# A streaming encoder layer on one core: roots turned on TensorE, a first load in two pieces, and another order in the last unit

## The chip, the cores and the metric

The kernel runs on one core of a Trainium2 chip. The metric is the device time of one execution in microseconds. Engine names: PE is TensorE (PEld its weight loads), DVE is VectorE, ACT is ScalarE, POOL is GpSimd, SP is SyncE. SP here does nothing but issue DMAs, in the order of its one queue; SPq and ACTq are the DMA-issuing sides of the engines.

## The reference

One layer for two groups of requests that share weights: a prompt of 2048 frames and 32 sample frames with cached state, width 1024, hidden width 2816, all in float32. In short:

```
h = RMSNorm(x); z = h @ W_in             # [pool u | q | f | i | g], 512 columns each
A = per-group map of (trailing mean over 2/4/8/16 frames - frame)
B = HGRN2 recurrence, 4 heads x 128, in chunks; per-head RMSNorm; SiLU(g) gate
x += RMSNorm(concat(A, B) @ W_out)
x += RMSNorm((SiLU(RMSNorm(x) @ W_gate) * (RMSNorm(x) @ W_up)) @ W_down)
outputs: y_prompt, y_sample, new pool rows and new states of both groups
```

The root of the first RMSNorm, 1 / sqrt(mean(x^2) + eps), is a number per frame. It is what the words "roots" below mean.

## The kernel before, in words

The prompt is worked off in two halves of 1024 frames; the sample frames ride with the second half. Each half goes through: values (the `i` columns), four heads (`head_products`, with the recurrence `hgrn` run as a background task), four pool groups, the output projection (`project`, in two token groups of 512), and the gate and up products (`gate_up`). After both halves the down products of both run in `down`.

Every float32 product is made from two rounded parts of each operand, high and low, as three matmuls (high x high, high x low, low x high); ACT casts the high part and DVE subtracts to get the low part. Gate, up and down use a seven-product scheme on 2 x 2 blocks: a unit has the products 1 to 7, and `order_of` writes down in which order they run. Products that share a PSUM bank (`u.x` of 1, 6, 5, 3; `u.y` of 7, 4) follow one another in it, each after DVE or ACT has read the last state. In `down` each unit adds its products into four quarters of two token tiles `acc[t]` and `acc[t + 4]`: product 2 completes the left half of tile t, 5 and 4 the two halves of tile t + 4, and 3 the right half of tile t. When both halves of a tile are complete, a root is taken on POOL and DVE scales both halves (`done`). For all units but the last the result is added to the output in DRAM by a POOL DMA; for the last unit DVE multiplies each completed half by the norm's weight (`fg`), scales it and adds the residual, and plain stores end the program.

What sets the order: PE's instructions are in the order of the program text, where background tasks (`Task`, `poll`) are stepped between matmuls by a clock of estimated PE time, `Pace.t`; a `yield n` asks for the next step n ns later. The queues of DVE, ACT, POOL and SP are ordered by a scheduler that estimates when each instruction is ready, so the same edit can move instructions on engines that it doesn't name. In the first values stage (`first_values`) the text sets the order of all engines.

Places that the change touches. `later_stats` (L466) takes the roots of the second half's 1024 frames during the first half: `st[:, 24:32]` holds them as 128 partitions x 8, and L489 stores them into the DRAM row `roots`, from where L521 broadcasts them to all partitions, hundreds of us later. `first_values` (L560) starts the program: 12 idle matmuls, the loads of x and of the first weights, and `unscaled` and `split`, which make the operands of the first products. `flush` (L1414) is the task that works off the hidden tiles' splits (`hidden`: `hhi`, `hlo`, `hs`) that are left when a half's gate and up products end. `gb` products are the small in-chunk products of a head, 64 in a group.

Of the kernel before, what the change touches and what calls it, by code (L numbers as in the profile page):

```python
# [16 lines left out]
P = 128  # L17
# [61 lines left out]
def body(tc, ins, outs, cst):  # L79
    nc = tc.nc  # L80
    ctx = ExitStack()
    with ctx:
# [113 lines left out]
        def tick(ns):  # L196
            Pace.t += ns
# [267 lines left out]
        def later_stats(S):  # L465

            st = S.st
            for i in range(NCH):
                for c in range(2):
                    x = t2("xtl")  # L470
                    r0 = S.tok0 + i * P
                    nc.sync.dma_start(out=x, in_=x_p[r0:r0 + P, c * 512:c * 512 + 512])
                    sumsq(x, P, st[:, 2 * i + c:2 * i + c + 1])
                    del x
                yield 20000.0
            xs = t2("xsl", [NS, 512]), t2("xsl", [NS, 512])
# [12 lines left out]
            nc.sync.dma_start(out=roots[0, 0:HALF].rearrange("(i p) -> p i", p=P), in_=st[:, 24:32])  # L489
            nc.sync.dma_start(out=roots[0, HALF:TMAX].rearrange("(p i) -> p i", i=1), in_=st[0:NS, 35:36])  # L490

        def scaled_channels(S, tg):
# [67 lines left out]
        def first_values(S):  # L560


            idle = small("idle", [P, 1], bufs=1)
            nc.scalar.activation(idle, ones[:, 0:1], AF.Copy)
            bank = axbank("idle")
            for _ in range(12):
                mm(bank[:, 0:P], ones, ones, True, True, 0.0)
            front_loads(S)
            S.xT[0] = [ztile("xT", [P, 2, 512]) for _ in range(4)]
            for kp in range(4):  # L570
                channel_load(S, 0, 2 * kp, 2 if kp else 1)
                raws(kp + 1)
                if kp == 0:
                    channel_load(S, 0, 1, 1)
            nc.sync.dma_start(out=cons[:, 0:C_VEC], in_=cst[:, 0:C_VEC])
            xg = {}

            def unscaled(k):
                x, c = S.xT[0][k // 2][:, k % 2], xtile("xg", [P, 2, 512])
                nc.scalar.activation(c[:, 0], x, AF.Copy, scale=g_pre[:, k:k + 1])  # L580
                nc.vector.scalar_tensor_tensor(c[:, 1], x, g_pre[:, k:k + 1], c[:, 0].bitcast(F32), ALU.mult, ALU.subtract)
                xg[k] = c[:, 0], c[:, 1]

            token_tiles(S, 1)
            S.xT[1] = [ztile("xT", [P, 2, 512]) for _ in range(4)]
            for kp in range(4):
                channel_load(S, 1, 2 * kp, 2)
                raws(kp + 5)
            token_tiles(S, 0)
            unscaled(0)  # L590
            ahead(1)
            unscaled(1)
            pss = value_tiles(S)
            for k in range(0, KD, 2):
                _, hi, lo = take(0)
                if k + 2 < KD:
                    unscaled(k + 2)
                    ahead(Stream.used + 1)
                    unscaled(k + 3)
                else:  # L600
                    ahead(Stream.used + 1)
                if k == 4:
                    token_stats(S, 1)
                for kk in range(2):
                    ah, al = xg.pop(k + kk)
                    if k + kk == 0:
                        for n, (a, b) in enumerate(((ah, hi[0]), (al, hi[0]), (ah, lo[0]))):
                            for i in range(4):
                                mm(pss[i], a[:, i * P:(i + 1) * P], b, n == 0, False, rcost(512))
                    else:  # L610
                        for i in range(4):
                            value_products(pss, i, ah, al, i * P, hi[kk], lo[kk], False, k + kk == KD - 1)
                    if k + kk == KD - 3:
                        later = scaled_channels(S, 1)
                        next(later)
                        next(later)
            for i in range(4):
                (nc.vector.tensor_copy if i % 2 else nc.scalar.copy)(S.vt[i], pss[i])
            pss = value_tiles(S)
            for k in range(0, KD, 2):  # L620
                _, hi, lo = take(0)
                next(later, 0)
                ahead(Stream.used + 1)
                if k == 2:
                    token_stats(S, 0, range(2))
                    next(later, 0)
                elif k == 4:
                    token_stats(S, 0, range(2, 4))
                    gate_bounds()
                elif k == 6:  # L630
                    for i in range(4):
                        if i % 2:
                            nc.vector.tensor_scalar(S.vt[i], S.vt[i], S.rs[0][i], None, ALU.mult)
                        else:
                            nc.scalar.activation(S.vt[i], S.vt[i], AF.Copy, scale=S.rs[0][i])
                for kk in range(2):
                    if k + kk == KD - 1:
                        earlier = scaled_channels(S, 0)
                        next(earlier)
                    ah, al = S.hT[k + kk]  # L640
                    for i in range(4):
# [493 lines left out]
        def order_of(n, lead):  # L1135
# [13 lines left out]
                    out += [(m - 1, 4), (m - 1, 3)]  # L1149
                out += [(m, 6), (m, 2), (m, 7), (m, 5)]  # L1150
            if not lead:
                return out + [(n - 1, 4), (n - 1, 3)]
            a, b = n - 2, n - 1
            return out + [(a, 1), (a - 1, 4), (a - 1, 3), (b, 1)] + [(m, p) for p in (6, 2, 7, 5, 4, 3) for m in (a, b)]

# [45 lines left out]
        def gate_up(S, on_last):  # L1201
# [212 lines left out]
            def flush():  # L1414
                while jobs:
                    job()
                    yield 1400.0

            Task(flush())

# [75 lines left out]
        def down(halves):  # L1496
# [38 lines left out]
            def half_done(t, dh, direct):  # L1535
                cs = slice(dh * 512, dh * 512 + 512)
                f = acc[t][:, cs]
                if t not in stats:
                    xh = None
                    if direct:  # L1540
                        xh = ztile("x1r", [P, D])
                        nc.sync.dma_start(out=xh, in_=x1_rows(t * P, P))
                    stats[t] = [new_stat(), [], xh]
                st, seen, xh = stats[t][0:3]
                sumsq(f, P, st[:, dh:dh + 1])
                seen.append(dh)
                if direct:
                    fg = t2("fg")
                    nc.vector.tensor_tensor(fg, f, gpf[0][:, cs], ALU.mult)
                    stats[t].append((dh, fg))  # L1550
                if len(seen) == 1:
                    first_half(st, P, dh)
                else:
                    rstd_of(st, P, True, nc.gpsimd, dh)
                    pending.append((slot[0] + (1 if direct else 4), lambda: done(t, direct)))

            def done(t, direct):
                f, rs, xh, fg = acc[t], stats[t][0][:, 3:4], stats[t][2], stats[t][3:]
                rows = slice(t * P, (t + 1) * P)
                for i in range(2):  # L1560
                    ds = slice(i * 512, i * 512 + 512)
                    if direct:
                        nc.vector.scalar_tensor_tensor(f[:, ds], dict(fg)[i], rs, xh[:, ds], ALU.mult, ALU.add)
                        (nc.scalar if i else nc.sync).dma_start(out=outs[0][0, rows, ds], in_=f[:, ds])
                    else:
                        nc.vector.scalar_tensor_tensor(f[:, ds], f[:, ds], rs, gpf[0][:, ds], ALU.mult, ALU.mult)
                if not direct:
# [182 lines left out]
```

## Time and profile before

| | |
|---|---|
| median of 3 runs | 2109.58 us (2109.41 to 2110.47) |
| profiled execution | 2110.55 us |
| its span | 2108.8 us |
| mean granted clock of TensorE | 0.996 |
| PE busy | 2081.5 us, 99% |
| PEld, DVE, ACT, POOL busy | 80%, 68%, 39%, 13% |
| DMA engines | 152 GB/s on the mean |

The rows below are of the profiled execution. Times are us from the start of its span. An instruction of a timeline has its start, its duration, its engine and line, what it writes and reads, and in brackets how long the engine stood idle before it and what ended that; "issue" means that nothing that the profile shows ended it. Consecutive like instructions are merged (x2, x64), with one duration for all.

### The profile page before, as it was taken

How to read it: one execution, taken by the hardware profiler on the slowest of the kernel's cores; microseconds unless marked ns; L12 is line 12 of the kernel's file. 1: busy time of each engine (PE TensorE's matmuls, PEld its weight loads, DVE VectorE, ACT ScalarE, POOL GpSimd, SP SyncE). 2: the span in 40 equal slices, each digit the busy share in tenths (PEclk: the TensorE clock that was granted, in tenths of full speed). 3: DMA queues.
4: the chain of work that ended last, by engine and by line, in shares of the span. 5: the costliest groups of instructions: out<-in, count | busy, mean ns of one | idle time of the engine just before them, and what ended most of it. 6: DMA issues, size and time to landing. Idle time of an engine off the chain costs nothing.

```text
span 2108.8 us, 34100 instructions
## 1 busy us (share of the span) xinstructions
PE 2081.5 (99%) x13117; PEld 1690.4 (80%) x13117; DVE 1423.5 (68%) x2302; ACT 831.6 (39%) x1659; POOL 283.4 (13%) x387
## 2 busy tenths in 40 slices
PE   9999899999999999999999999999999999999998
PEld 8788688888888887778878788888888778888876
DVE  6565575797777778456575687767666856566587
ACT  6444344654444445233333664444444521011032
POOL 1132302200000000022231210000000301110134
PEclk9999999999999999999999999999999999999999
DMA  9321142626555557310014524545455796776778
GB/s 322 111 72 51 34 150 96 194 86 176 162 155 155 150 175 229 112 45 25 23 36 162 188 93 130 156 141 148 147 148 151 241 311 207 225 225 196 223 224 215
DMA packets 394242, 321.07 MB, mean 152 GB/s; under 512 B 19144, under 2 KB 321472, under 8 KB 394080
## 3 DMA queue, kind: packets, MB, share of 16 engines
q1 hardware_dynamic: 391632, 310.98, 47.9%
q0 software_dynamic: 2016, 7.34, 1.9%
q8 instruction: 104, 1.70, 0.3%
q10 hardware_dynamic: 432, 0.57, 0.1%
q14 instruction: 58, 0.48, 0.1%
HBM read 218.36 MB, written 100.47 MB: 151 GB/s over the span
## 4 chain that ended last, share of the span: by engine, by line
PE 88%; DVE 6%; issue 2%; DMA 1%; ACT 1%; POOL 1%; SPq 0%; DVEq 0%; POOLq 0%; ACTq 0%
PE gx L200 21%; PE mmb L200 15%; PE gy L200 10%; PE dx L200 10%; PE ops L200 10%; PE gz L200 5%; PE dy L200 5%; PE vps L200 3%; PE dz L200 2%; PE gb L200 1%; DVE acc L1533 1%; PE gw L200 1%; PE gsps L200 1%; PE ups L200 1%; PE tps L343 1%
## 5 line engine op out<-in xcount | busy, mean ns | idle before, releaser
L200 PE MATMUL gx<-fhi,wf 128*128 128x512 f32 x1376 | 387.3, 391 | 0.0
L200 PEld LDWEIGHTS gx<-fhi,wf 128*128 128x128 f32 x1376 | 256.6, 188 | 55.3 <-issue 3.0
L200 PE MATMUL gx<-flo,wf 128*128 128x512 f32 x688 | 213.0, 390 | 0.0
L200 PE MATMUL gy<-fhi,wf 128*128 128x512 f32 x704 | 201.8, 390 | 0.1
L200 PE MATMUL dx<-dhi,hst 128*128 128x512 f32 x640 | 185.3, 391 | 0.8 <-DVE acc L1533 0.6
L200 PE MATMUL mmb<-hTlo,whi 128*128 128x512 f32 x512 | 177.4, 407 | 0.0
L200 PE MATMUL mmb<-hThi,whi 128*128 128x512 f32 x512 | 166.4, 406 | 5.6 <-issue 5.6
L1533 DVE TENSOR_TENSOR acc<-dx,acc 128x512 f32<-128x512 f32 x168 | 115.0, 689 | 72.9 <-PE dx L200 72.1
L1256 DVE TENSOR_TENSOR wf<-s,wf 128x512 fp32r<-128x512 f32 x176 | 119.9, 687 | 60.6 <-ACT wf L1251 58.3
L200 PE MATMUL mmb<-hThi,wlo 128*128 128x512 f32 x512 | 159.9, 394 | 0.0
L200 PEld LDWEIGHTS gy<-fhi,wf 128*128 128x128 f32 x704 | 131.7, 188 | 28.5 <-DVE c L1355 0.8
L200 PEld LDWEIGHTS gx<-flo,wf 128*128 128x128 f32 x688 | 129.1, 188 | 27.0
L1251 ACT CAST wf<-s 128x512 fp32r<-128x512 f32 x176 | 108.3, 621 | 102.5 <-DVE s L1232 31.5
L200 PEld LDWEIGHTS dx<-dhi,hst 128*128 128x128 f32 x640 | 119.5, 188 | 30.0 <-issue 3.4
L1256 DVE TENSOR_TENSOR wf<-wraw,wf 128x512 fp32r<-128x512 f32 x132 | 89.6, 686 | 40.2 <-ACT wf L1251 40.2
L200 PEld LDWEIGHTS mmb<-hThi,whi 128*128 128x128 f32 x512 | 91.6, 189 | 27.3 <-issue 10.0
L200 PEld LDWEIGHTS mmb<-hTlo,whi 128*128 128x128 f32 x512 | 96.6, 189 | 21.1 <-issue 1.3
L200 PEld LDWEIGHTS mmb<-hThi,wlo 128*128 128x128 f32 x512 | 96.9, 189 | 19.5 <-issue 0.7
L1472 ACT CAST dhi<-t 128x1024 fp32r<-128x1024 f32 x20 | 20.6, 1052 | 232.2 <-DVE dlo L1473 163.7
L1251 ACT CAST wf<-wraw 128x512 fp32r<-128x512 f32 x132 | 80.8, 621 | 73.9 <-PE gx L200 37.4
L200 PE MATMUL gy<-flo,wf 128*128 128x512 f32 x352 | 108.7, 389 | 0.0
L200 PE MATMUL dy<-dhi,hst 128*128 128x512 f32 x320 | 98.6, 389 | 1.1 <-DVE acc L1533 1.1
(327 smaller groups left out, 3998.0 us busy)
## 6 DMA issues: line engine op xcount, KB each, us to landing
hst<-hdFalse SPq DMA_DIRECT2D x140, 256.0 KB, 3.0
hst<-hdTrue SPq DMA_DIRECT2D x140, 256.0 KB, 3.0
wraw<-in_w_gate_dram SPq DMA_DIRECT2D x50, 512.0 KB, 4.2
wraw<-in_w_up_dram SPq DMA_DIRECT2D x50, 512.0 KB, 4.0
hdFalse<-hhi SPq DMA_DIRECT2D x77, 256.0 KB, 2.3
hdFalse<-hlo SPq DMA_DIRECT2D x77, 256.0 KB, 2.5
hdTrue<-hhi SPq DMA_DIRECT2D x77, 256.0 KB, 2.6
hdTrue<-hlo SPq DMA_DIRECT2D x77, 256.0 KB, 2.5
```

The costliest lines, as they stand in the source:

```text
L200: nc.tensor.matmul(out, l, r, start=start, stop=stop, skip_group_check=more)
L343: nc.tensor.transpose(ps[:, c:c + P], xn[:, (2 * kp + kk) * P:(2 * kp + kk + 1) * P], ident)
L1251: nc.scalar.copy(wf[:, 0], getattr(M, src) if isinstance(src, str) else src)
L1256: nc.vector.tensor_tensor(wf[:, 1], getattr(M, src) if isinstance(src, str) else src, wf[:, 0].bitcast(F32), ALU.subtract)
L1472: nc.scalar.copy(hi, src)
L1533: nc.vector.tensor_tensor(dst, ps, dst, ALU.add)
```

## The change

Four edits. The roots of the second half are transposed by TensorE from 128 x 8 to 8 x 128, copied by ACT, and stored as 8 rows. At the start the first x load is cut into two loads of 256 columns with the first weight block between them, the operands of the first product are made in that order, and there are 9 idle matmuls instead of 12. The last unit of `down` runs its products as 6, 7, 5, 4, 2, 3 instead of 6, 2, 7, 5, 4, 3, and the two scalings of a finished tile are due in two slots instead of one. The flush asks for 2800 ns between steps instead of 1400.

```diff
@@ later_stats
-            nc.sync.dma_start(out=roots[0, 0:HALF].rearrange("(i p) -> p i", p=P), in_=st[:, 24:32])
+            yield 3000.0
+            ps = axbank("rps")
+            nc.tensor.transpose(ps[0:NCH, 0:P], st[:, 24:32], ident)
+            tick(107)
+            rows = t2("rows", [NCH, P])
+            nc.scalar.copy(rows, ps[0:NCH, 0:P])
+            nc.sync.dma_start(out=roots[0, 0:HALF].rearrange("(i p) -> i p", p=P), in_=rows)
@@ first_values
-            for _ in range(12):
+            for _ in range(9):
                 mm(bank[:, 0:P], ones, ones, True, True, 0.0)
...
+                nc.sync.dma_start(out=S.xT[0][0][:, 0, 0:256], in_=x0[:, 0:256])
...
+                for i in range(2):
+                    nc.sync.dma_start(out=raw[:, i * 512:(i + 1) * 512], in_=w_in[i * P:(i + 1) * P, COL_I:COL_I + 512])
+                    if i == 0:
+                        nc.sync.dma_start(out=S.xT[0][0][:, 0, 256:512], in_=x0[:, 256:512])
+                    else:
+                        channel_load(S, 0, 1, 1)
...
-            unscaled(0)
-            ahead(1)
+            unscaled(0, slice(0, 256))
...
+            nc.scalar.copy(h[:, 0:512], raw[:, 0:512])
+            unscaled(0, slice(256, 512))
+            nc.vector.tensor_tensor(l[:, 0:512], raw[:, 0:512], h[:, 0:512].bitcast(F32), ALU.subtract)
+            nc.scalar.copy(h[:, 512:1024], raw[:, 512:1024])
+            nc.vector.tensor_tensor(l[:, 512:1024], raw[:, 512:1024], h[:, 512:1024].bitcast(F32), ALU.subtract)
@@ order_of
-                return out + [(n - 1, 4), (n - 1, 3)]
+                return out[:-4] + [(n - 1, p) for p in (6, 7, 5, 4, 2, 3)]
@@ flush
-                    yield 1400.0
+                    yield 2800.0
@@ half_done, done
-                    pending.append((slot[0] + (1 if direct else 4), lambda: done(t, direct)))
+                    for i in range(2):
+                        wait = 1 if direct else i + (3 if t % 8 > 3 else 4)
+                        pending.append((slot[0] + wait, lambda i=i: done(t, direct, i)))
```

What the edits move, first on SP. These are its rows before around the store of the roots, in the first half's last head; `xtl` and `xsl` are the frames whose roots are taken, `wraw` and `wrow` weights.

```order
L472 DMA xtl<-in_x_prompt_dram 128x512 x2
L489 DMA roots<-st_b 128x8x1
L251 DMA wraw<-in_w_in_dram 128x8x128
L258 DMA wrow<-in_w_out_dram 128x2x512
L478 DMA xsl<-in_x_sample_dram 32x512 x2
L490 DMA roots<-st_b 32x1
```

The first of the two `roots` rows is gone from there. Now it stands in the second token group of the first half's projection; SP's rows of the changed kernel there, with `xr` the residual's rows and `ym` the layer's intermediate result:

```order
L258 DMA wrow<-in_w_out_dram 128x2x512
L495 DMA roots<-rows 8x128
L251 DMA wraw<-in_w_gate_dram 128x8x128
L251 DMA wraw<-in_w_up_dram 128x8x128
L251 DMA wraw<-in_w_gate_dram 128x8x128
L251 DMA wraw<-in_w_up_dram 128x8x128
L251 DMA wraw<-in_w_gate_dram 128x8x128
L251 DMA wraw<-in_w_up_dram 128x8x128
L1127 DMA xr<-in_x_prompt_dram 128x512 x2
```

Before, two `xr` loads stood in the place of `roots<-rows`, and six more came behind the gate and up loads.

Second, ACT in the second half's values stage, where `hThi` are casts of the normed input, `hhi` casts of the flush, and `va`, `vb` copies that free the banks of finished values. Before:

```order
L507 CAST hThi_7458<-xT 128x512
L507 CAST hThi_7460<-xT 128x512
L507 CAST hThi_7462<-xT 128x512
L1178 CAST hhi<-hs 128x512
L670 COPY va<-vps 128x512
L670 COPY vb<-vps 128x512
```

The same place in the changed kernel:

```order
L513 CAST hThi_7462<-xT 128x512
L1208 CAST hhi<-c_7355 128x512
L513 CAST hThi_7464<-xT 128x512
L700 COPY va<-vps 128x512
L513 CAST hThi_7466<-xT 128x512
L700 COPY vb<-vps 128x512
```

The copy `va` now stands ahead of the last cast `hThi`, and no `hhi` stands between them.

Third, DVE at the end of the program, from the add of product 6 on (`dx` is the bank of 6, 5 and 3, `dy` that of 7 and 4, `dz` that of 2). Before:

```order
L1533 TENSOR_TENSOR acc<-dx,acc 128x512
L1566 SCALAR_TENSOR_TENSOR acc<-acc,st,gv 128x512
L1533 TENSOR_TENSOR acc<-dz,acc 128x512
L1566 SCALAR_TENSOR_TENSOR acc<-acc,st,gv 128x512
L1549 TENSOR_TENSOR fg<-acc,gv 128x512
L1533 TENSOR_TENSOR acc<-dy,acc 128x512
L1533 TENSOR_TENSOR acc<-dx,acc 128x512
L1549 TENSOR_TENSOR fg<-acc,gv 128x512
L1533 TENSOR_TENSOR acc<-dy,acc 128x512
L1549 TENSOR_TENSOR fg<-acc,gv 128x512
L1533 TENSOR_TENSOR acc<-dx,acc 128x512
L1563 SCALAR_TENSOR_TENSOR acc<-fg,st,x1r 128x512
```

There follow another `fg` and three scalings L1563. The changed kernel from its add of product 7 on:

```order
L1563 TENSOR_TENSOR acc<-dy,acc 128x512
L1594 SCALAR_TENSOR_TENSOR acc<-acc,st,gv 128x512
L1563 TENSOR_TENSOR acc<-dx,acc 128x512
L1578 TENSOR_TENSOR fg<-acc,gv 128x512
L1563 TENSOR_TENSOR acc<-dy,acc 128x512
L1578 TENSOR_TENSOR fg<-acc,gv 128x512
L1563 TENSOR_TENSOR acc<-dz,acc 128x512
L1591 SCALAR_TENSOR_TENSOR acc<-fg,st,x1r 128x512
L1578 TENSOR_TENSOR fg<-acc,gv 128x512
L1591 SCALAR_TENSOR_TENSOR acc<-fg,st,x1r 128x512
L1563 TENSOR_TENSOR acc<-dx,acc 128x512
L1578 TENSOR_TENSOR fg<-acc,gv 128x512
```

Two scalings L1591 follow. The last add, of product 3, stood ahead of all four scalings of the last two tiles and now stands behind two of them.

## Rows read from the trace of the kernel before

**Rows 1.** Whom PE waited for in the whole span: us, times, longest.
```profile
PE mmb L200 <- issue: 5.6, 1, 5.6
PE gb L200 <- issue: 3.5, 2, 3.1
PE vps L200 <- ACT va L670: 2.3, 1, 2.3
...
PE dx L200 <- ACT acc L1528: 0.7, 1, 0.7
PE dx L200 <- DVE acc L1533: 0.6, 2, 0.5
```

**Rows 2.** PE's timeline, groups of small products in two consecutive heads.
```profile
189.59 0.73 PE L200 MATMUL gb<-qa,k_t 128*32 128x16 f32 x64 [0.35 <-DVE qa L802]
192.51 0.89 PE L200 MATMUL gb<-qa,k_t 128*32 128x16 f32 x64
...
236.16 0.44 PE L200 MATMUL gb<-qa,k_t 128*32 128x16 f32 x31 [0.35 <-issue]
...
250.58 0.75 PE L200 MATMUL gb<-qa,k_t 128*32 128x16 f32 x64
```

**Rows 3.** Windows: PE, PEld, DVE, ACT, POOL busy; granted clock, DMA share, GB/s.
```profile
238.00:240.00 2.00, 0.18 (x1) 0.00 (x0) 0.00 (x0) 0.00 (x0) 0.00 (x0) 1.00 0.28 18
...
242.00:244.00 2.00, 0.09 (x1) 0.00 (x0) 1.42 (x2) 0.00 (x0) 0.27 (x1) 0.50 1.00 348
```

**Rows 4.** SP's timeline, the store of the roots.
```profile
229.30 0.38 SPq L489 DMA_DIRECT2D roots<-st_b  x1
```

**Rows 5.** DMA: queues 184 to 196, then 224 to 244 with issues; page.
```profile
q1 hardware_dynamic: 144, 0.26, 6.8%
q8 instruction: 3, 0.05, 1.7%
...
q1 hardware_dynamic: 2292, 0.95, 24.9%
...
wraw<-in_w_in_dram SPq DMA_DIRECT2D x1, 512.0 KB, 14.2
...
wraw<-in_w_in_dram SPq DMA_DIRECT2D x32, 512.0 KB, 5.3
```

**Rows 6.** SP's timeline at the first gate weights; chain of waits, first gate product.
```profile
368.24 0.39 SPq L251 DMA_DIRECT2D wraw<-in_w_gate_dram  x1
...
390.24 5.44 PE gx L200 x24
```

**Rows 7.** Timelines of ACT and PE, the first operand and the first product.
```profile
4.49 0.72 ACT L580 ACTIVATE xg<-xT,cons 128x512 fp32r<-128x512 f32 x1 [1.83 <-DMA cons<-shape_constants]
...
5.77 2.14 PE L200 MATMUL vps<-whw,xg 128*128 128x512 f32 x8
```

**Rows 8.** Chain of waits in the second half's values stage: start, us, what.
```profile
836.61 0.59 ACT va L670
...
837.25 12.79 PE vps L200 x48
...
851.03 11.11 PE vps L200 x48
```

**Rows 9.** Timelines of DVE and PE at the end of the program.
```profile
2093.59 0.68 DVE L1533 TENSOR_TENSOR acc<-dx,acc 128x512 f32<-128x512 f32 x1
...
2097.45 0.74 PE L200 MATMUL dy<-dhi,hst 128*128 128x512 f32 x2 [1.06 <-DVE acc L1533]
...
2099.14 0.69 DVE L1533 TENSOR_TENSOR acc<-dy,acc 128x512 f32<-128x512 f32 x1 [0.22 <-PE dy L200]
...
2100.50 0.69 DVE L1533 TENSOR_TENSOR acc<-dx,acc 128x512 f32<-128x512 f32 x1
2101.76 0.75 DVE L1563 SCALAR_TENSOR_TENSOR acc<-fg,st,x1r 128x512 f32<-128x512 f32 x1 [0.57 <-POOL st L327]
...
2104.22 1.41 DVE L1563 SCALAR_TENSOR_TENSOR acc<-fg,st,x1r 128x512 f32<-128x512 f32 x2 [0.44 <-POOL st L327]
```

**Rows 10.** Chain of waits at the first down units.
```profile
1703.27 3.02 DMA hdTrue<-hlo
```

More of the change, by code (lines that the diff above doesn't have):

```diff
@@ L570, in first_values, with unscaled @@
             for kp in range(4):
[L571 to L574, printed above, removed]
+                if kp:
+                    channel_load(S, 0, 2 * kp, 2)
+                    raws(kp + 1)
+                    continue
+                x0 = x_t[:, 0, S.tok0:S.tok0 + 512]
+                nc.sync.dma_start(out=S.xT[0][0][:, 0, 0:256], in_=x0[:, 0:256])
+                raw = ztile("wrow", [P, 2 * 512])
+                Stream.items[0] = lambda: raw
+                for i in range(2):
[4 more added lines that the diff above has]
+                        channel_load(S, 0, 1, 1)
+                raws(1)
             nc.sync.dma_start(out=cons[:, 0:C_VEC], in_=cst[:, 0:C_VEC])
             xg = {}
[L578 to L582, printed above, removed]
+            def unscaled(k, cs=slice(0, 512)):
+                x = S.xT[0][k // 2][:, k % 2]
+                if k not in xg:
+                    xg[k] = xtile("xg", [P, 2, 512])
+                hi, lo = (xg[k][:, i, cs] for i in range(2))
+                nc.scalar.activation(hi, x[:, cs], AF.Copy, scale=g_pre[:, k:k + 1])
+                nc.vector.scalar_tensor_tensor(lo, x[:, cs], g_pre[:, k:k + 1], hi.bitcast(F32), ALU.mult, ALU.subtract)
             token_tiles(S, 1)
@@ L589, in first_values @@
             token_tiles(S, 0)
-            unscaled(0)
-            ahead(1)
+            unscaled(0, slice(0, 256))
+            raw = Stream.items[0]
+            h, l = xtile("whw", [P, D]), xtile("wlw", [P, D])
+            nc.scalar.copy(h[:, 0:512], raw[:, 0:512])
[3 more added lines that the diff above has]
+            nc.vector.tensor_tensor(l[:, 512:1024], raw[:, 512:1024], h[:, 512:1024].bitcast(F32), ALU.subtract)
+            Stream.items[0] = raw, [h[:, 0:512], h[:, 512:1024]], [l[:, 0:512], l[:, 512:1024]]
+            Stream.nsplit = 1
+            raws(1 + LOOKRAW)
+            del raw
             unscaled(1)
@@ L604, in first_values @@
                 for kk in range(2):
-                    ah, al = xg.pop(k + kk)
+                    ah, al = (xg[k + kk][:, i] for i in range(2))
+                    del xg[k + kk]
                     if k + kk == 0:
@@ L1542, in half_done @@
                         nc.sync.dma_start(out=xh, in_=x1_rows(t * P, P))
-                    stats[t] = [new_stat(), [], xh]
-                st, seen, xh = stats[t][0:3]
+                    stats[t] = [new_stat(), [], xh, [t2("fg") for _ in range(2)] if direct else None]
+                st, seen, xh, fg = stats[t]
                 sumsq(f, P, st[:, dh:dh + 1])
@@ L1547, in half_done @@
                 if direct:
-                    fg = t2("fg")
-                    nc.vector.tensor_tensor(fg, f, gpf[0][:, cs], ALU.mult)
-                    stats[t].append((dh, fg))
+                    nc.vector.tensor_tensor(fg[dh], f, gpf[0][:, cs], ALU.mult)
                 if len(seen) == 1:
@@ L1554, in half_done, with done @@
                     rstd_of(st, P, True, nc.gpsimd, dh)
-                    pending.append((slot[0] + (1 if direct else 4), lambda: done(t, direct)))
[L1557 to L1567, printed above, removed]
+                    for i in range(2):
+                        wait = 1 if direct else i + (3 if t % 8 > 3 else 4)
+                        pending.append((slot[0] + wait, lambda i=i: done(t, direct, i)))
+            def done(t, direct, i):
+                f, (st, _, xh, fg) = acc[t], stats[t]
+                rs, rows, ds = st[:, 3:4], slice(t * P, (t + 1) * P), slice(i * 512, i * 512 + 512)
+                if direct:
+                    nc.vector.scalar_tensor_tensor(f[:, ds], fg[i], rs, xh[:, ds], ALU.mult, ALU.add)
+                    (nc.scalar if i else nc.sync).dma_start(out=outs[0][0, rows, ds], in_=f[:, ds])
+                    return
+                nc.vector.scalar_tensor_tensor(f[:, ds], f[:, ds], rs, gpf[0][:, ds], ALU.mult, ALU.mult)
+                if i:
                     nc.gpsimd.dma_start(out=outs[0][0, rows, :], in_=f, accum_op=ALU.add)
```

## The prediction

> **What bounds the kernel now.** I read the page's busy table first: TensorE (PE) is busy for 99% of the span, so only two things can move the time, idle PE time and PE time at the lower clock. Next the list of who PE waited for. Its two largest entries name nobody: 5.6 us before a projection product and 3.5 us before small head products, both "issue", PE ready to run with no semaphore outstanding [rows 1]. The other entries are 2.3 us on a ScalarE (ACT) copy and pieces of about 1 us or less. So the reader looks for the place of the nameless ones. The PE timeline puts both between 236 and 248 us. In each head the `gb` products come in groups of 64 with nine big products between groups. In the head before, two such groups start at 189.59 and 192.51, 2.92 us apart; the same pair in this head starts at 236.16 and 250.58, 14.42 us apart [rows 2]. [...] At 229.30 SyncE (SP) had issued the store of `roots` from `st[:, 24:32]`: 1024 single floats [rows 4]. The weight load issued behind it landed after 14.2 us, where its kind takes 5.3. The queue that brings PE's instructions delivered three blocks in the 12 us from 184 to 196, and none in the 20 us from 224 to 244: its line is missing there [rows 5]. My reading is that the single-float store clogs the DMA engines, PE runs out of fetched instructions and stops.
>
> **Part by part.** The sum is made against the profiled execution, 2110.55 us (span 2108.8 us); the median of the three timed runs is 2109.58, 0.97 below.
>
> *Roots through TensorE.* The 1024 floats become a transpose, an ACT copy of 8 rows, and a store of 8 rows of 512 bytes. In the new program SP no longer has that store at 229 us; the only small one left there is the second, 32 floats. If the clog goes, the pair of groups is 2.92 apart again: 14.42 - 2.92 = **-11.5 us**, which holds the idle time and the products at the low clock together. The smallest gain that I would book to the store is the idle time in front of the `gb` groups alone, 3.5 us [rows 1]; the largest is the 11.5, since the head before runs through the same loop with nothing removable in it.
>
> The transpose itself moves far. It is ordered by TensorE's order, so it lands in the second output projection (367 us in the old times), and the store goes with it. On PE it is one small product; a product of 512 columns takes 11.11 / 48 = 0.23 us [rows 8], so at most +0.2, taken as **+0.1**. Its PSUM bank was last read three transposes earlier, so I expect no wait. What is queued behind it matters more: SP now has `roots<-rows` just ahead of the first nine gate and up weight loads and waits there for the ACT copy. In the old trace SP was held by the `xr` loads and sent the first of these weights at 368.24; the copy can run at about 369, and the first product that needs the weights is at 390.24 [rows 6]. A load of 5.3 and a split of two operations of about 0.7 each leave some 14 us. Cost **0**, hidden by the projection's products; a loss begins if the copy comes later than about 383. Four weight splits of the projection are also moved behind the evacuations of its first half. Each still has several us before its products, so 0 to +2, taken as 0.
>
> *First load in pieces.* The old start: ACT scales 512 columns at 4.49, casts the first weights, PE starts at 5.77 [rows 7]. Now ACT scales 256 columns (0.72 becomes an estimated 0.4), then casts. ACT's start at 4.49 is set by the small constants' load, not by x, so it does not come earlier. Gain 0.3. Nine idle products instead of twelve leave PE about half a us idle before the start; if the clock then rises later, the 16 or so first products at twice their time could lose 1 us or more. I take **-0.3**, between -0.5 and +1.5.
>
> *Flush at half the rate.* After the first half's gate and up, leftover splits of its hidden tiles run on DVE and ACT beside the second half's norm. PE waits there for ACT's copy `va` at 836.61; it starts at 837.25 and its 48 products take 12.79 us, where the next 48 take 11.11 [rows 8], so the place costs 2.3 + 1.7 = 4.0 us. The new ACT order puts `va` ahead of the last `hThi` cast and has no `hhi` in front of it; DVE has one leftover operation fewer in front of the last `xT` scalings, 0.7 us. So the copy can begin when PE finishes, about 835, done 835.6. But DVE's own copy of the second bank now stands behind a weight split and a leftover, and I count it at 838.4: PE runs one group (6 x 0.23 = 1.4 us) and waits another 1.4. Together 0.7 + 1.4 = 2.1 in two pieces. The 1.06 us of idle time at the end of the program were followed by products at full rate [rows 9], so I expect no clock loss. That is -1.9 at best, nothing at worst; taken **-1.5**. At the start of the down products the same thinning takes DVE work out of the first units, whose waits are 0.7 and 0.6 [rows 1], and puts it into later ones: **-0.3**, between -1 and +0.7.
>
> *Last unit in another order, 6 7 5 4 2 3.* Old: product 4 waits 1.06 us for DVE and starts at 2097.45 [rows 9]. New: product 5 comes one place earlier and accumulates into the bank that product 6 left; DVE's add of 6 starts at 2093.59 and takes 0.68, so 5 starts at about 2094.3, 4 at 2095.7, 1.75 earlier, and its add at 2099.14 - 1.75 = 2097.4. That is where the gain ends. DVE's new order runs the two scalings of the finished tile and one `fg` ahead of the last add. The first scaling starts 2101.76 - 2099.14 = 2.62 after the add of 4, at 2100.0; with three operations of 0.65 the last add starts at 2101.95, where it was 2100.50. From last add to last pair of scalings it took 3.72 (2104.22 - 2100.50); with GpSimd undisturbed, as in the chain before, 2.62. So the last pair starts at 2104.6 to 2105.7 instead of 2104.22: **+0.4**, up to +1.5; if DVE reaches the last add without waiting it would be -1.
>
> *Scaling in two slots.* DVE's order before the last unit is the same, so 0.
>
> Sum: -11.5 + 0.1 - 0.3 - 1.5 - 0.3 + 0.4 = **-13.1**. From the profiled execution 2097.45, from the median 2096.5. I take **2096.6**, since the median is what will be compared.
>
> **Rivals.**
>
> *Only part of the stall belongs to the store (B).* For it: the longer idle stretch, 5.6 us, goes on while the large loads rush through at 348 GB/s [rows 1, 3], so an instruction block may have stood behind those and not behind the floats. Against it: the loads were only that late because of the store, and the head before has large loads too and no such idle time. Price: the 5.6 and the half-rate products around them (some 2 us) stay, so the change brings 13.1 - 7.6 = 5.5: 2104.1.
>
> [...]
>
> *The store is not the cause (C).* The head simply runs out of instructions here. For it: the groups consume instructions fastest of all. Against it: the head before does the same with 2.92 us. Only the small terms are left, -1.6: 2108.0.
>
> *Slower (D).* In the first units of the down products SP's one line carries the leftovers' stores (`hdTrue`) and the loads (`hst`) of the coming units. The old chain of waits already runs through such a store, 3.02 us at 1703.27 [rows 10]. At half the rate the 14 leftover steps, 1.4 us apart before, last some 20 us longer, and a store that waits for its split holds every load behind it. If the cover of the loads is used up, as that chain hints, PE stands still for up to these 20 us: 2096.6 + 20 = 2116.6. It decides from a hold of 13 us, which eats the whole gain. Against it: the new SP order puts more loads ahead of the late stores than the old one.
>
> **How the numbers follow.** Forecast 0.77, B 0.12, C 0.08, D 0.03. The forecast's own range by the bounds of the small terms is 2094 to 2100.5. To leave out no more than 2 in 10 the range goes on into B: 2094.0 to 2102.0. What can be told from no change is about 0.2%, 4.2 us, so below 2105.4 is faster: the forecast and nearly all of B, 0.88. Same: C and the edge of B, 0.09. Slower: D, 0.03.
>
> **What will show it.** Right: the `gb` groups of the last head of the first half about 2.9 us apart, instruction blocks arriving between them, the granted clock at 1.00 there, the load behind landing in about 5 us; PE's nameless idle time gone from the wait list. For the flush: the wait for `va` under 1 us, perhaps a new one for DVE's copy. For the end: PE finishing earlier, the last add later than before relative to PE, the span's end unmoved or worse. Wrong: idle "issue" time still there without the floats (C), or half of it (B); PE waiting for `hst` loads after 1690 (D); SP late with the gate weights and PE idle near 390; the first products at half rate (the start).

## The result, and the profile after

| | before | after |
|---|---|---|
| median | 2109.72 us (4 runs, 2109.41 to 2110.47) | 2096.92 us (4 runs, 2095.99 to 2098.40) |
| profiled execution, its span | 2110.55, 2108.8 us | 2095.99, 2094.2 us |
| granted clock, mean | 0.996 | 0.999 |
| PE busy | 2081.5 us | 2077.2 us |

The ratio is 0.9938, 95% interval 0.9926 to 0.9950: 12.8 us faster, where 2096.6 us had been forecast. The changed kernel was timed again with the experiments: 2097.04 us against 2108.28, ratio 0.9947 [0.9933, 0.9960]. The two traces differ by 14.6 us of span, more than either pair of medians, because the profiled execution of before lay near the upper end of its kernel's runs, which in the later comparisons went from 2104.34 to 2111.07.

I read the views in the same order as before. The list of whom PE waited for, kernel after (us, times, longest), answers to [rows 1]: both nameless entries are gone, and so is the wait for `va`. A new one stands second, `gy` waiting for DVE (`gx`, `gy`, `gz` and `gw` are banks of the gate and up products).

```profile
PE gb L200 <- DVE qa L832: 1.9, 5, 0.7
PE gy L200 <- DVE c L1385: 1.4, 2, 0.8
PE idle L200 <- POOL cmps L145: 1.0, 1, 1.0
PE dx L200 <- DVE acc L1563: 0.8, 2, 0.7
PE dx L200 <- ACT acc L1558: 0.7, 1, 0.7
```

PE's timeline of the same groups of small products, against [rows 2]:

```profile
189.85 0.82 PE L200 MATMUL gb<-qa,k_t 128*32 128x16 f32 x64 [0.35 <-DVE qa L832]
192.88 0.74 PE L200 MATMUL gb<-qa,k_t 128*32 128x16 f32 x64
...
236.31 0.73 PE L200 MATMUL gb<-qa,k_t 128*32 128x16 f32 x64 [0.33 <-DVE qa L832]
239.23 0.74 PE L200 MATMUL gb<-qa,k_t 128*32 128x16 f32 x64
```

The pair of the last head is 239.23 - 236.31 = 2.92 us apart, as in the head before; it was 14.42. The windows, against [rows 3], show PE full and the granted clock at 1.00, where it had been 0.50:

```profile
238.00:240.00 2.00, 2.00 (x71) 1.50 (x70) 1.90 (x2) 0.00 (x0) 0.74 (x1) 1.00 0.03 8
242.00:244.00 2.00, 2.00 (x40) 1.43 (x39) 0.76 (x3) 0.17 (x1) 1.31 (x4) 1.00 0.01 0
```

The DMA queues from 224 to 244 have an instruction line again, three blocks, against [rows 5]. (q8 is taken for PE's queue by its share: in before it brings 1.70 of the 2.18 MB of both instruction queues, 78%, and PE has 26234 of the 34100 instructions, 77%.)

```profile
q1 hardware_dynamic: 399, 0.62, 9.0%
q8 instruction: 3, 0.05, 0.9%
```

SP's timeline from 225 to 250 has only the samples' loads and the second store left, against [rows 4]. The two weight loads that stood behind the store at 229.73 and 230.40 are now issued ahead of that place, at 216.66 and 222.67.

```profile
227.38 0.81 SPq L478 DMA_DIRECT2D xsl<-in_x_sample_dram  x2
242.72 0.31 SPq L496 DMA_DIRECT2D roots<-st_b  x1
```

The new store runs in the projection. SP's timeline, then the chain of waits at the first gate product (against [rows 6]): SP sends the store at 357.29 and the first gate weight 0.44 us later; that product starts 21 us after.

```profile
357.29 0.34 SPq L495 DMA_DIRECT2D roots<-rows  x1
357.73 0.40 SPq L251 DMA_DIRECT2D wraw<-in_w_gate_dram  x1
```

```profile
374.90 4.08 PE ops L200 x18
378.98 5.44 PE gx L200 x24
```

The values stage of the second half, chain of waits from 800 to 850, against [rows 8]: PE runs through 144 products in one piece; the wait and the slow 48 products are both gone.

```profile
802.59 32.64 PE vps L200 x144
835.23 0.99 PE vsps L200 x8
836.22 11.11 PE vps L200 x48
```

For a reckoning by stage I took from both PE timelines the time of the same product; each row has what the stretch took after, less what it took before, in us. "Again" is the second trace of the changed kernel.

| stretch (times of before) | forecast | after | again |
|---|---|---|---|
| start to 107.77 (first head) | -0.3 | +0.32 | +0.69 |
| to 200.99 (third head) | 0 | -0.13 | -0.10 |
| to 258.92 (the stall) | -11.5 | -11.58 | -11.52 |
| to 390.07 (first gate product) | +0.1 | +0.14 | +0.13 |
| to 813.20 (gate and up) | 0 | +0.64 | +0.66 |
| to 862.14 (values) | -1.5 | -4.20 | -4.20 |
| to 1662.60 (first down product) | 0 | +0.90 | +0.62 |
| to 1771.36 (first down units) | -0.3 | -0.95 | -0.90 |
| to the end | +0.4 | +0.26 | +0.32 |
| sum | -13.1 | -14.60 | -14.30 |

### The profile page after: what moved, and what is told of

Same layout as the page of the kernel before. It is cut to its first block, busy times and chain, and to the rows that moved or that the text cites. A ratio compares the mean times of both kernels' runs of the same rounds, so it can differ in the third digit from the quotient of the medians.

```text
span 2094.2 us, 34086 instructions
## 1 busy us (share of the span) xinstructions
PE 2077.2 (99%) x13112; PEld 1689.3 (81%) x13112; DVE 1425.1 (68%) x2303; ACT 832.5 (40%) x1661; POOL 282.0 (13%) x387
## 4 chain that ended last, share of the span: by engine, by line
PE 90%; DVE 5%; DMA 1%; issue 1%; ACT 1%; POOL 1%; SPq 0%; DVEq 0%; POOLq 0%; ACTq 0%
PE gx L200 22%; PE mmb L200 15%; PE gy L200 11%; PE dx L200 10%; PE ops L200 10%; PE gz L200 5%; PE dy L200 5%; PE vps L200 3%; PE dz L200 3%; PE gb L200 1%; PE gw L200 1%; DVE acc L1563 1%; PE gsps L200 1%; PE ups L200 1%; PE tps L343 1%
## 5 line engine op out<-in xcount | busy, mean ns | idle before, releaser
L1563 DVE TENSOR_TENSOR acc<-dx,acc 128x512 f32<-128x512 f32 x168 | 115.1, 689 | 71.7 <-PE dx L200 71.0
L200 PE MATMUL dx<-dlo,hst 128*128 128x512 f32 x320 | 98.8, 390 | 0.0
```

The lines of the kernel that those rows point to most:

```text
L200: nc.tensor.matmul(out, l, r, start=start, stop=stop, skip_group_check=more)
L1563: nc.vector.tensor_tensor(dst, ps, dst, ALU.add)
```

## The experiments

The kernel before, timed beside them, had medians of 2108.31 us (first four), 2107.46 (next four) and 2108.28 (last four).

**1. The roots alone.** The `later_stats` part of the diff, on the kernel before.

> The kernel before with the roots edit alone (transpose on TensorE, copy, store of 8 rows). Whole-stall theory (the single floats hold the instruction fetch until the last of them): the two gb groups of the last head are 2.9 us apart, 11.5 us are gained and 0.1 is paid for the transpose, 2098.3 us. Rival B (only a part of the stall belongs to the floats): 5.5 us gained, 2104.2. Rival C (the head runs out of instructions by itself): 2109.7.

2098.54 us, ratio 0.9954 [0.9939, 0.9969]. The stall is gone: from 200.99 to 258.92 this trace saves 11.56 us, and no nameless wait of PE is left. C falls. B isn't tested cleanly here, since the two weight loads behind the store also move ahead, to 216.18 and 222.19; experiment 2 decides it. Two waits of `gy` for DVE (1.6 us in all) are there that before did not have.

```profile
235.84 0.73 PE L200 MATMUL gb<-qa,k_t 128*32 128x16 f32 x64 [0.33 <-DVE qa L808]
238.74 0.74 PE L200 MATMUL gb<-qa,k_t 128*32 128x16 f32 x64
```

```profile
PE gy L200 <- DVE c L1361: 1.6, 2, 1.0
```

**2. The same bytes in wider pieces.**

```diff
-nc.sync.dma_start(out=roots[0, 0:HALF].rearrange("(i p) -> p i", p=P), in_=st[:, 24:32])
+nc.sync.dma_start(out=roots[0, 0:HALF].rearrange("(p i) -> p i", p=P), in_=st[:, 24:32])
```

> The kernel before with its store of the roots at the same place of the same queue, the same 4096 bytes, but as 128 pieces of 32 bytes in place of 1024 of 4 (the roots then stand in another order in DRAM, so that the second half's frames get each other's roots). Whole-stall theory: what counts is the number of pieces, the stall goes as with the roots edit, 2098.2 us, and the load issued behind lands in about 5 us. Rival B: the large loads behind still stand before the instruction blocks, 2104.2. Rival C: 2109.7.

2095.94 us, ratio 0.9945 [0.9930, 0.9960]. SP's order is that of before, the store stands at 229.09, and the load issued behind it lands in 4.0 us instead of 14.2. So neither the store's place nor its bytes made the stall, and the large loads behind it (B) don't make it by themselves. DMA issues, 224 to 262:

```profile
wraw<-in_w_in_dram SPq DMA_DIRECT2D x1, 512.0 KB, 4.0
...
roots<-st_b SPq DMA_DIRECT2D x1, 4.0 KB, 1.4
```

**3. Half of the floats.** Four of the eight columns as 512 floats, the others as 128 pieces of 16 bytes. The 12.7 us in the expectations of this run and the next lie between the store's issue at 229.30 [rows 4] and the window from 242 us, with its 348 GB/s [rows 3].

> The kernel before with half of the roots stored as 512 single floats and the other half as 128 pieces of 16 bytes (those again in another order in DRAM). Whole-stall theory: the engines are clogged for about half of the 12.7 us, so some 6.3 us are gained, 2103.4 us, or all 11.5, 2098.2, if PE's fetched instructions last that long. [...] Rival C: 2109.7.

2107.21 us, ratio 0.9995 [0.9986, 1.0005]: no difference that can be told. The load behind lands after 12.3 us. PE's waits:

```profile
PE mmb L200 <- issue: 6.3, 1, 6.3
PE gb L200 <- issue: 2.4, 4, 1.1
```

**4. The floats twice.** A second store of the same 1024 floats, into another row.

> The kernel before with the store of single floats issued twice, the second time into a spare row of DRAM that nothing reads: 2048 floats. Whole-stall theory: another 12.7 us of clog, all of them PE idle, 2122.4 us, with the weight load behind landing after some 27 us. [...] Rival C: 2109.7.

2115.31 us, ratio 1.0036 [1.0023, 1.0049]: 7.0 us slower, less than the 2122.4 of the whole-stall theory and more than the 2109.7 of rival C. The load behind lands after 21.4 us.

```profile
PE gb L201 <- issue: 10.7, 4, 8.0
PE mmb L201 <- issue: 4.6, 1, 4.6
```

The landing times 4.0, 12.3, 14.2 and 21.4 us for 0, 512, 1024 and 2048 floats are no straight line, so a clog in step with the number of floats doesn't fit. (The kernel with 512 also stores 128 pieces of 16 bytes side by side; what those cost by themselves wasn't tried.) I looked at the DMA queues of before again, first 230 to 231, then 231 to 241 (packets, MB, share of 16 engines):

```profile
q1 hardware_dynamic: 1042, 0.01, 48.0%
```

```profile
q1 hardware_dynamic: 369, 0.19, 20.3%
```

All the floats' packets are over within one microsecond. What is slow are the ten behind it: 369 packets of the large loads in 10 us, 19 GB/s, with the engines 20% busy. In the kernel with wide pieces the same window moves 1330 packets, 117 GB/s. So something that the floats left behind held up all later traffic.

The trace's semaphore events, which the views don't list, say what was left: the store itself. Each complete DMA there shows 16 completion signals. The store of experiment 2 has all 16 within 1.4 us of its issue. Of the stores of floats side by side only a part of the signals is on record (in before none), and they are late: in this one three of the first store at 236.4 to 236.9 and four of the second at 246.6 to 248.1, 17.4 to 18.9 us after its issue; in experiment 3 two at 238.4 to 238.7. Here the traffic goes from 54 to 264 GB/s at 249, in experiment 3 from 70 to 266 at 241. As far as the record goes, then, the hold-up lasts about as long as the floats' writes are unfinished. Why these writes take so long isn't shown.

The same traces show what PE's last stop waits for. Before the same product of the projection PE stands idle in before and in experiments 3, 4 and 5, in this order:

```profile
247.72 1.22 PE L200 MATMUL mmb<-hThi,whi 128*128 128x512 f32 x2 [5.63 <-issue]
246.69 1.22 PE L200 MATMUL mmb<-hThi,whi 128*128 128x512 f32 x2 [6.31 <-issue]
253.71 1.22 PE L201 MATMUL mmb<-hThi,whi 128*128 128x512 f32 x2 [4.56 <-issue]
239.00 0.73 PE L201 MATMUL mmb<-hThi,whi 128*128 128x512 f32 x2 [0.74 <-issue]
```

In each of the four the next block of PE's instruction queue comes just ahead: it is in at 246.24, 245.20, 252.49 and 237.80, and PE goes on 1.2 to 1.5 us later. The block before it had come between 223 and 226. In the traces without single floats there the same block starts between 232 and 236, and PE doesn't stop. So that stop is PE out of instructions. The first stop, 3.12 us before 239.72 in before, is not explained by this: it ends, in the middle of a group of 64, while no block arrives (225 to 245). In this experiment it is the longer one (10.7 us in four pieces). What ended it stays open.

**5. The floats far apart.** The 32-byte store in the right order (see 7), and behind it 1024 floats 256 bytes apart.

```diff
+spare = DP.tile([1, 64 * HALF], F32, name="spare")
...
+far = spare[0, :].rearrange("(i p s) -> p i s", p=P, s=64)[:, :, 0:1]
+nc.sync.dma_start(out=far, in_=st[:, 24:32].rearrange("p (i s) -> p i s", s=1))
```

> The roots loaded so that partition p holds frames 8p to 8p+7 and stored as 128 pieces of 32 bytes (which gives them in the right order), and behind that store another of 1024 single floats from the same source, each 256 bytes from the next in a spare DRAM row that nothing reads. [...] Theory of the piece (each write of 4 bytes is slow, wherever it goes): the stall as in the kernel before, PE idle some 9 us with nothing to wait for, some 2108 us.

2101.28 us (2098.24 to 2103.87), ratio 0.9971 [0.9962, 0.9981]. As many single floats, from the same tile, at the same place: in the profiled execution the load behind lands in 5.6 us, and one nameless wait of 0.7 us is left. DMA issues and PE's wait:

```profile
wraw<-in_w_in_dram SPq DMA_DIRECT2D x1, 512.0 KB, 5.6
...
spare<-st_b SPq DMA_DIRECT2D x1, 4.0 KB, 3.2
```

```profile
PE mmb L201 <- issue: 0.7, 1, 0.7
```

In this execution, then, most of the stall is gone, and the theory of the piece doesn't fit it. But it (2098.31) was among the fastest here: its trace shows 1.0 us of delay in the last head of the first half and 0.9 before it, while the median is 4.4 us above the kernel of 7, which has no floats, and the slowest run 7.0. The slower the run, the lower its mean granted clock: 0.999 up to 2100.85 us, 0.998 or 0.997 above, with 0.997 in the two slowest, where the runs of before, with the stall, have 0.995 to 0.997. So the slower runs may well have had a part of the stall; none of them has a trace. What is shown is that floats far apart do less harm than floats side by side, not that they do none, and not at what distance it ends: only 4 and 256 bytes were tried.

**6. Floats where PE is not hungry.** The changed kernel, with its `rows` stored once more as single floats, side by side, ahead of the gate loads.

```diff
+nc.sync.dma_start(out=spare[0, 0:HALF].rearrange("(p i) -> i p", i=NCH), in_=rows)
```

> The changed kernel with one more store of the same 1024 roots as single floats, into a spare DRAM row that nothing reads, right behind its store of 8 rows: it runs in the output projection, ahead of the first gate and up loads. Theory of the starved PE (the floats hold up everything in the DMA engines, and PE stops only where it needs instructions fast): the loads behind land after 13 us or more, but PE shows no nameless wait there, since a product of 512 columns takes 0.23 us and one of 16 columns 0.012; 2097 us, or a wait of 0 to 2 us for the gate weights on top. Rival (a store of single floats stops PE wherever it is): some 9 us idle near 370, 2108.

2098.66 us, ratio 0.9959 [0.9946, 0.9973]. The traffic behind the store is held up again, 754 packets from 361 to 369, where 5260 go in the changed kernel's trace; the first gate weight lands after 13.1 us, and the part of this store's completion signals that is on record runs to 367.7. PE has no nameless wait; it waits once, for a copy of `ym` (the chain of waits leads to a store of `ym` that took 4.40 us; experiment 11, without these floats, has 0.7 us of the same wait behind a residual load):

```profile
PE tps L344 <- ACT ym L1122: 1.6, 1, 1.6
```

From 352 to 390 a single instruction block arrives on PE's queue, and PE goes on without another: each of its products takes 0.23 us there, where in the head 64 products of 16 columns take 0.74 us. The theory of the starved PE holds, with the 1.6 us on top.

**7 and 8. Roots in the right order without a transpose; and the flush on top.** Tile i of the statistics loads the frames 8p + i, so that the 32-byte pieces are in order.

```diff
-r0 = S.tok0 + i * P
-nc.sync.dma_start(out=x, in_=x_p[r0:r0 + P, c * 512:c * 512 + 512])
+xr = x_p[S.tok0:S.tok0 + HALF, c * 512:c * 512 + 512].rearrange("(p i) c -> i p c", i=NCH)
+nc.sync.dma_start(out=x, in_=xr[i])
```

> The kernel before with the roots in 128 pieces of 32 bytes in the right order: tile i of the statistics loads the frames 8p + i instead of 128 i + p, so that no transpose is needed. If the floats are the cause and the transpose on TensorE costs something (the two waits of products for DVE that showed with the roots edit alone, 1.6 us), 2096.5 us, some 2 us below the roots edit alone, and no worse than the changed kernel. If the transpose is free and the difference was between executions: 2098.

> The same with the flush's 2800 ns. Forecast of the prediction for the flush: 1.8 us less than without, 2094.7. Rival (the wait in the values stage differs from execution to execution, and most of what the flush seemed to gain there is that): within 0.5 us of the run without, 2096 to 2096.5.

2096.83 us, 0.9949 [0.9936, 0.9961], and with the flush 2095.00, 0.9942 [0.9930, 0.9955]. The flush is worth 1.8 us, with a small overlap of the runs (2095.75 to 2097.67, 2094.21 to 2096.01). Its traces say where. From the last gate product to the end of the values stage, PE takes 44.7 us in all seven traces with 2800 ns, and 45.2 to 46.1 in six with 1400 beside the 48.94 of the profiled execution of before; from the first down product to 1771 it takes 0.8 to 0.95 us less than before in the seven and 0 to 0.2 less in the six. PE's wait for `va` with 1400 was 0.2 to 1.0 us in the six, and none with 2800.

```profile
PE vps L200 <- ACT va L670: 0.4, 1, 0.4
```

That is the kernel of 7. The wait of `gy` at 435 us, 0.62 us, stands in all the traces with the transpose (the two of the changed kernel, 1, 6, 10 and 11) and in none without it (before, 2 to 5, 7, 8, 12); 5 and 12 have one of 0.4 and 0.5 us later, between 750 and 815 us. The ratios of 7 (0.9949) and of the roots edit alone (0.9954) have overlapping intervals, so what the transpose costs is told by the traces and not by the medians.

**9 to 11. The changed kernel again, with the old start, and with the old last unit.**

> The changed kernel itself once more, beside the next three. All theories: 2097 us. A term of the prediction that is only in one execution would show as a difference of its trace from the first one of the same kernel: the first trace had no wait for a copy in the second half's values stage, and the runs of the kernel before differ there by up to 4 us.

> The changed kernel with the start of the kernel before (first load in one piece, 12 idle products). The prediction's term, -0.3 for the new start: 0.3 us slower than the changed kernel. Reading of the trace after (first product 0.6 earlier, but the products of the first weights 0.7 later by 49 us and 0.3 later by 96 us): 0.3 to 0.7 us faster than the changed kernel, and the idle wait for the mixing weights at 90 us longer.

> The changed kernel with the last unit in the old order 6 2 7 5 4 3, the two slots kept. The prediction's term, +0.4 for the new order: 0.4 us faster than the changed kernel, DVE's last add about 1.5 us earlier against the down products, PE's last product 0.4 later. Rival (the end follows PE): 0.4 slower.

The changed kernel 2097.04 us (2096.23 to 2098.29); with the old start 2094.91 (2094.66 to 2095.31), ratio to before 0.9935 [0.9923, 0.9948]; with the old last unit 2095.83 (2095.60 to 2096.32), 0.9940 [0.9928, 0.9953]. The old start is better by 2.1 us, no run overlapping. Of that the two traces show 1.27 us by the first head and 0.5 between the values and the down products; what the new start has to do with the latter isn't shown. Over all traces the first head comes 0.7 us later with the new start (mean +0.51 of four, against -0.22 of ten). ACT's and PE's timelines, changed kernel:

```profile
3.98 0.51 ACT L600 ACTIVATE xg<-xT,cons 128x256 fp32r<-128x256 f32 x1 [1.32 <-DMA cons<-shape_constants]
...
5.79 0.62 ACT L615 CAST whw<-wrow 128x512 fp32r<-128x512 f32 x1 [0.27 <-DMA wrow<-in_w_in_dram]
```

```profile
5.17 2.59 PE L200 MATMUL vps<-whw,xg 128*128 128x512 f32 x8
...
11.92 0.50 PE L200 MATMUL vps<-wlw,xg 128*128 128x512 f32 x1 [0.22 <-DVE wlw L238]
```

PE starts 0.60 us sooner than in [rows 7], but the eight first products take 2.59 us instead of 2.14. The trace's record of the granted clock begins with a 1.00 (the windows show nothing of the time ahead of it): at 4.87 in before, among the idle products, which are 0.213 us apart until then and 0.112 behind it, so that the clock rises there, and at 6.20 here, behind the first products, which are 0.59 and 0.43 us apart. Of its lead of 0.60 PE has 0.16 left behind the eighth product. In the three other traces with the new start the clock rises at 4.82, 5.60 and 6.37, and 0.58, 0.39 and 0.07 us are left. The larger loss comes later, where the loads land later: ACT casts the next weights at 10.52 (10.77 in the second trace) instead of 9.05, or 9.45 in experiment 10. In the trace shown PE waits for their low part at 11.92, in the second one for the second operand `xg`, and by 49 us the changed kernel is 0.73 and 1.04 us behind before, experiment 10 only 0.05.

The end, DVE's timeline of the changed kernel (against [rows 9]):

```profile
2085.21 0.75 DVE L1591 SCALAR_TENSOR_TENSOR acc<-fg,st,x1r 128x512 f32<-128x512 f32 x1 [0.60 <-POOL st L327]
...
2087.15 0.68 DVE L1563 TENSOR_TENSOR acc<-dx,acc 128x512 f32<-128x512 f32 x1
...
2089.74 1.42 DVE L1591 SCALAR_TENSOR_TENSOR acc<-fg,st,x1r 128x512 f32<-128x512 f32 x2 [1.19 <-POOL st L327]
```

and with the old last unit:

```profile
2086.16 0.69 DVE L1563 TENSOR_TENSOR acc<-dx,acc 128x512 f32<-128x512 f32 x1
...
2089.88 1.41 DVE L1591 SCALAR_TENSOR_TENSOR acc<-fg,st,x1r 128x512 f32<-128x512 f32 x2 [0.44 <-POOL st L327]
```

Counted from the last `sacc` group (the samples' down products) at about 1991 us, 2006 in before, the last pair of scalings starts after 98.40 us in both traces of the changed kernel, and after 98.07 with the old unit (98.02 before). The new order costs 0.35 us; the other 0.9 between the medians is not its own.

**12. All of it together.** Kernel 8, the new last unit, and `done` one slot later, which puts DVE's last add ahead of the second scaling.

> The roots in 128 pieces of 32 bytes in the right order (no transpose), the flush's 2800 ns, the old start, and the last unit in the new order with the finished tile's scalings due one slot later, so that DVE's last add stands ahead of the second of them. Against the run with the first two alone (2095.0): 0.3 us less, 2094.7; some 2 us below the changed kernel. Rival (the transpose costs nothing and the runs only differ): as the changed kernel, 2097.

2095.71 us (2094.35 to 2096.29), ratio 0.9937 [0.9925, 0.9950]. The end does what was meant: the last pair of scalings starts 97.88 us after `sacc`, 0.14 sooner than before. But this execution lost 1.5 us at its first product, where the others with this start lost 0.4 or less, and the gains below a microsecond can't be told from that. So the forecast of 2094.7 wasn't reached. By their ratios to the kernel before beside them, the changed kernel with the old start (0.9935), this one (0.9937) and kernel 8 (0.9942) can't be told apart; the first also beats the changed kernel beside it.

## Why the prediction was right, and where it was not

*The stall: right in place and size.* 14.42 - 2.92 = 11.5 was forecast, 11.50 to 11.58 is what every trace without single floats in that head shows (1, 2, 6 to 12 and the changed kernel's first). Taking the whole distance between two like groups, instead of adding up idle time, caught the products at the low clock (0.50 in [rows 3]) as well.

*How the stall comes about: half wrong.* "The single-float store clogs the DMA engines" holds in its effect only. The float packets were through in a microsecond, and the engines then were 20% busy; what was late were the completions of the store's writes (up to 18.9 us after the issue in experiment 4). As many floats, 256 bytes apart, left 0.7 us of nameless wait in the execution that was traced. That PE runs out of instructions is shown for its last stop, by the block that comes 1.2 to 1.5 us before PE goes on in four traces, and fits experiment 6; what ended the first stop is open. Why writes of floats side by side take so long stays open too: no view here looks behind the DMA engines.

The size of a write alone doesn't make the stall: the 32-byte pieces and the floats 256 bytes apart are small too, and the loads behind them landed in 4.0 and, in the traced execution, 5.6 us. Nor do the floats' packets themselves: in before they were over by 231, and the next instruction block started at 245.24, some 14 us later.

*Transpose: +0.1 forecast, +0.8 found.* The product itself cost the 0.14, and the loads behind the new store were early enough. The 0.64 is a wait for DVE's read of the bank `gy` (before, after, and PE after):

```profile
444.36 0.68 DVE L1355 TENSOR_TENSOR c<-gy,c 128x512 f32<-128x512 f32 x1
434.15 0.68 DVE L1385 TENSOR_TENSOR c<-gy,c 128x512 f32<-128x512 f32 x1
434.98 0.70 PE L200 MATMUL gy<-fhi,wf 128*128 128x512 f32 x2 [0.62 <-DVE c L1385]
```

PE is 11.25 us earlier than before there, this read only 10.21, so it is 1.04 us late. DVE's order changed around the end of the projection, and from 403 us on it runs 0.74 us late against PE. That fits what I had put at "0 to +2, taken as 0", the moved DVE work in the projection; which of the moved operations it was wasn't tried.

*Start: wrong sign.* Of "ACT's start at 4.49 is set by the small constants' load, not by x, so it does not come earlier" the first half held, but that load landed earlier too, and ACT started 0.51 us earlier. The condition "if the clock then rises later" came true in three of the four traces with the new start, at a cost of 0.1 to 0.5 us, where I had allowed 1 us or more (its 16 slow products were an estimate; the trace shown has two gaps of 0.59 and 0.43 us, then at most 0.25); it did so in one trace with the old start too (experiment 5, at 6.46), so that the missing idle products made it isn't shown. The rest of the loss comes with the later loads, which the text did not follow. 0.7 us lost is within the stated +1.5.

*Flush: right by the runs, wrong by the trace.* 1.8 us was forecast and 1.8 came. But the prediction took the wait of 2.3 us in the profiled execution as the kernel's own. In six other traces with the same 1400 ns it is 0.2 to 1.0. The new worry, a wait for DVE's copy of the second bank, never came; the smaller gain in the values (0.9) and the larger one in the down products (0.8, forecast 0.3) made up the sum by luck.

*The end: right.* +0.4 forecast, +0.35 measured, by the step named: the last add moved behind two scalings, from 2100.50 to 2087.15 + 14.86 = 2102.01 in the old times, where 2101.95 was forecast. PE finished 0.37 earlier, and it brought nothing.

*The sum: near by luck.* With the sizes that were found, -11.5 + 0.8 + 0.7 - 1.7 + 0.35 is -11.35, smaller by 1.7 us than the -13.1 of the forecast, and the later comparison of the same two kernels found as much: 2108.28 - 2097.04 = 11.2. That 2096.6 was met within half a microsecond is owed to the median that it was counted from: 2109.58, of three runs, lies 1.3 above the 2108.28 of the nine later ones. The 4.0 us that the prediction saw at the values stage, too, were one execution's.

*Not foreseen:* 0.6 to 0.9 us between the values and the down products; in the first trace 0.8 of it is a wait of `gy` at 1637 us, which some executions have (up to 1.0 us) and others not, in the second 0.5 arise between 1200 and 1250 us. D did not happen: no `hst` load stands among PE's waits, and a store like that of [rows 10] is no longer in the chain of waits there.

## What to carry to other kernels

An idle time that nobody ended, among the smallest products of a kernel, is a reason to look at the instruction queue's line in the DMA view, and then at what was stored just before. Store a column of statistics so that each partition writes its numbers in one run, by choosing which rows a partition loads: behind pieces of 32 bytes the next load landed in 4.0 us here, behind single floats in 14.2, and it adds no instruction, where a transpose on TensorE added one and went with 0.64 us of other waiting. A wait of 2 us in one profiled execution is a size to be bounded by other executions before it goes into a sum.

## What the runs showed of the hardware

- 1024 single floats stored side by side in DRAM held nearly all later DMA traffic to some 19 GB/s for ten microseconds, the fetch of instructions included (no block on q8 from 225 to 245); behind 2048 it was 22 GB/s from 231 to 241, and 264 came only at 249. 32-byte pieces side by side did not (load behind: 4.0 us). Floats 256 bytes apart hardly did in the one execution traced (5.6 us), but their runs lay 1.4 to 7.0 us above the median of the kernel without them. At what distance or width it stops wasn't tried.
- A store's packets being over does not mean that the store is: in experiment 4 the packets of the 2048 floats were over within some 2 us, and completion signals of their stores came up to 18.9 us after the issue.
- The floats side by side stopped PE where 64 products took 0.74 us; in front of products of 0.23 us (experiment 6) they cost late loads, 13.1 us for the first, and one wait of 1.6 us.
